# Padding three SBUF pools of a two-layer encoder so that matmul operands begin at multiples of 512 bytes

## The chip, the cores and the metric

The kernel runs on one core of one Trainium2 chip. The metric is the device time of one execution in microseconds (us), here the median of three runs. [...]

## The reference

Two layers, each a half-step SwiGLU, a mixer, and another half-step SwiGLU, on 512 tokens of 1024 values in float32:

```python
for l in range(DEPTH):                                   # DEPTH = 2
    x = x + 0.5 * swiglu_ffn(rmsnorm(x, ffn1_norm[l]), ffn1_w_up[l], ffn1_w_down[l])
    x = x + mixer(rmsnorm(x, mix_norm[l]), w_in[l], ...)
    x = x + 0.5 * swiglu_ffn(rmsnorm(x, ffn2_norm[l]), ffn2_w_up[l], ffn2_w_down[l])
    x = rmsnorm(x, final_norm[l])

def swiglu_ffn(h, w_up, w_down):                         # 1024 -> 2 x 2816 -> 1024
    a, b = jnp.split(h @ w_up, 2, axis=-1)
    return (jax.nn.silu(a) * b) @ w_down
```

The mixer makes one projection of 8704 columns (q, k, v of three groups of eight heads, a gated input of a convolution, two branch gates), runs a banded attention in each group, a depthwise convolution over 31 tokens with LayerNorm, a projection of each branch, their gated sum and an output projection.

## The kernel before

The activations are kept transposed, 128 channels on the partitions and 512 tokens along the free dimension, in eight tiles `x0` to `x7`. A float32 product is made of three products of parts rounded to `float32r`: `mm3` (lines 165 to 168) multiplies upper by upper, upper by lower and lower by upper part, into one PSUM bank. `nc.tensor.matmul(ps, a, b)` loads `a` as the stationary operand (the LDWEIGHTS rows on PEld) and streams `b` past it (the MATMUL rows on PE).

The weights come through `stage` (lines 152 to 163): a DMA on the SP queue into `raw`, a rounded copy `hi` on ScalarE (line 161), and `lo` = raw - hi on VectorE (line 162). They are tiles of 128 x 1024 of the pool `wp`, sliced in steps of 128 or 256 columns, that is of 512 or 1024 bytes. The streamed operands of 512 columns are whole tiles:

- `xgh`, `xgl` (the normalized input of an FFN or a mixer) and `zh`, `zl` in the pool `xp`. They are streamed in the up-projections (`ps_a`, `ps_b`), the gated input (`ps_ga`, `ps_gg`), the gates (`ps_gc`, `ps_gA`) and the convolution's projection (`ps_cp`);
- `sh`, `sl` in the pool of the FFN, or of the mixer, streamed in the down-projections (`ps_d`) and the attention's projection (`ps_ap`);
- `sgc` (upper) and `ml` (lower part of the merged branches) in the mixer's pool, streamed in the output projection (`ps_o`).

For q, k and v (`tokens_chunk`, lines 320 to 337) it is the other way round: slices of 128 columns of `xgh`, `xgl` are stationary, and 256 columns of `hi` or `lo` are streamed into `ps_n`, 24 matmuls and one of the bias (line 336) for every 128 tokens. The attention transposes tiles by matmuls with the identity `ident` as the streamed operand (lines 396 and 479).

Pools take SBUF in the order in which they are opened, each behind the last, and a pool's tiles stand one behind the other in the order in which their tags first come: `const` (identity, ones, small parameters, masks, `sel`), `xp`, `wp`, `rp` (small rows and columns, `R`), and then one at a time the pool `x0` of the start, the pool of each FFN and the pool `mp` of each mixer. The tiles `tmp`, `rt3`, `big` and `gqk` stand at the start of `mp`; behind `trash` come `tab`, `bias`, `qk`, `sgc`, `V`, `ot` and `sp`. All of these but `trash` are whole multiples of 512 bytes.

The order of the instructions on each engine is fixed when the program is built, by priorities and a simulated timeline; `stage` runs ahead of its use. On TensorE the work of the attention, the gates and the projections is mixed in that order.

Of the kernel before, what the change touches and what calls it, by code (L numbers as in the profile page):

```python
# [11 lines left out]
F32 = mybir.dt.float32  # L12
# [4 lines left out]
PSUM = bass.MemoryType.PSUM  # L17
DRAM = bass.MemoryType.DRAM

P = 128  # L20
# [5 lines left out]
HD = 64  # L26
# [5 lines left out]
CW = 31  # L32
CH = 256            # columns of q, k or v at a time: four heads
UH = CH // HD
FF = 2816
# [9 lines left out]
def trunk(ctx: ExitStack, tc: tile.TileContext, A: dict, out: bass.AP):  # L45
    nc = tc.nc
    const = ctx.enter_context(tc.tile_pool(name="const", bufs=1))
    xp = ctx.enter_context(tc.tile_pool(name="xp", bufs=1))
    wp = ctx.enter_context(tc.tile_pool(name="wp", bufs=4))
    rp = ctx.enter_context(tc.tile_pool(name="rp", bufs=2))  # L50
# [11 lines left out]

# [1 line left out]
    ident = const.tile([P, P], F32, name="ident")  # L64
# [7 lines left out]

    # input, natural layout
    x0s = ExitStack()
# [35 lines left out]
    nc.gpsimd.dma_start(sel32, A["sel"])  # L110
    sel = const.tile([96, 4, P], F32R, name="sel")
    nc.vector.tensor_copy(sel, sel32)
    # the biases of q, k, v as rows of three parts, in DRAM
    NB3 = DEPTH * 3 * AW // CH
# [29 lines left out]

# [1 line left out]
    cnt = [0]  # L146

    def uniq(s):
        cnt[0] += 1
        return f"{s}_{cnt[0]}"  # L150

    def stage(src):
        """Weights [128, a, n] into their upper and lower 12 bits."""
        a, n = src.shape[1], src.shape[2]
        raw = wp.tile([P, 1024], F32, tag="raw", name=uniq("raw"), bufs=2)
        hi = wp.tile([P, 1024], F32R, tag="hi", name=uniq("hi"))
        lo = wp.tile([P, 1024], F32R, tag="lo", name=uniq("lo"))
        m = a * n
        with tc.high_priority(offset=150):
            nc.sync.dma_start(raw[:, :m].rearrange("p (a n) -> p a n", a=a), src)  # L160
            nc.scalar.activation(hi[:, :m], raw[:, :m], AF.Copy)  # L161
            nc.vector.tensor_sub(lo[:, :m], raw[:, :m], hi[:, :m].bitcast(F32))  # L162
        return (hi[:, :m].rearrange("p (a n) -> p a n", a=a), lo[:, :m].rearrange("p (a n) -> p a n", a=a))
# [6 lines left out]
    def split(pool, src, tag, bufs):  # L170
        """A tile's upper and lower 12 bits."""
        return split_to(pool.tile([P, S], F32R, tag=tag, name=uniq("sh"), bufs=bufs), pool.tile([P, S], F32R, tag=tag, name=uniq("sl"), bufs=bufs), src)
# [39 lines left out]
    def broadcast_psum(rc, pool):  # L212
        """[128 tokens, 4] columns as a row over all partitions."""
        dg = pool.tile([P, S], F32, tag="tmp", name=uniq("dg"), bufs=7)
        for tt in range(TT):
            nc.vector.tensor_scalar_mul(dg[:, tt * P:(tt + 1) * P], ident, rc[:, tt:tt + 1])
        ps = ps_st(uniq("ps_bc"))
        nc.tensor.matmul(ps, ones, dg, start=True, stop=True)
        return ps
# [7 lines left out]
    def proj_cols(src, c0, rhs, nk, ps):  # L227
        """ps[j] = src[:, c0 + 128 j ..].T @ rhs, one or two tiles of columns."""
        nj = len(ps)
        step = 8 // nj  # L230
        for kk in range(0, nk, step):
            n_ = min(step, nk - kk)
            wh, wl = stage(src[:, kk:kk + n_, c0:c0 + nj * P])
            for j in range(nj):
                for k in range(n_):
                    kg = kk + k
                    mm3(ps[j], wh[:, k, j * P:(j + 1) * P], wl[:, k, j * P:(j + 1) * P], *rhs[kg], kg == 0, kg == nk - 1)

# [1 line left out]
    def ffn(l, w_up, w_down, xg, R, after, deferred=None):  # L240
# [30 lines left out]

# [1 line left out]
    def mixer(l, xg, R, rc, after):  # L273
# [5 lines left out]
        with ExitStack() as mx:  # L279
            mp = mx.enter_context(tc.tile_pool(name=uniq("mix"), bufs=2))  # L280
# [3 lines left out]

            # 1 / r as a row of three parts, and eps / r^2
            rr, rt = rc
            e4 = rp.tile([P, TT], F32, tag="e4", name=uniq("e4"))
            nc.vector.scalar_tensor_tensor(e4, rt, EPS, rt, op0=ALU.mult, op1=ALU.mult)
            ps = ps_st(uniq("ps_rt"))
# [8 lines left out]

# [1 line left out]
            u = [None] * KD  # L300
# [15 lines left out]

# [1 line left out]
            # one set of tables for the logarithms and the exponentials that follow  # L318
            tc.keep_in_program_order(nc.scalar.preload_act_table_set("natural_log_exp_and_others"))
            def tokens_chunk(c0):  # L320
                """256 columns of z over r, tokens on partitions: two PSUM banks of two tiles of tokens."""
                ps = [ps_mm(uniq("ps_n")) for _ in range(2)]
                w = [stage(win[:, kk:kk + 4, c0:c0 + CH]) for kk in (0, 4)]
                b3 = mp.tile([3, CH], F32R, tag="bias", name=uniq("bias"), bufs=2)
                nc.gpsimd.dma_start(b3, bd[(l * 3 * AW + c0) // CH])
                for tt in range(TT):
                    ts = slice(tt * P, (tt + 1) * P)
                    o = ps[tt // 2][:, (tt % 2) * CH:(tt % 2 + 1) * CH]
                    for k in range(KD):
                        wh, wl = w[k // 4][0][:, k % 4], w[k // 4][1][:, k % 4]  # L330
                        xh, xl = xg[k]
                        nc.tensor.matmul(o, xh[:, ts], wh, start=k == 0, stop=False)  # L332
                        nc.tensor.matmul(o, xh[:, ts], wl, start=False, stop=False)  # L333
                        nc.tensor.matmul(o, xl[:, ts], wh, start=False, stop=False)  # L334
                    # the bias, over the scale that the rows still lack
                    nc.tensor.matmul(o, rt3[:, ts], b3, start=False, stop=True)  # L336
                return ps

            # q carries the scores' factor, k its sign: the scores come out negated
            gqk = mp.tile([P, 2, NG, HD], F32, tag="gqk", name=uniq("gqk"), bufs=1)  # L340
            for i, (nm, f) in enumerate((("q_norm", SCALE), ("k_norm", -1.0))):
# [3 lines left out]
                nc.vector.tensor_scalar_mul(gqk[:, i], gqk[:, i], f)  # L345
            trash = mp.tile([P, HD], F32, tag="trash", name=uniq("trash"), bufs=1)

# [8 lines left out]
            def qk_chunk(g, hh, qk, tab):  # L356
                """Norm, rotation and transpose of four heads of q (0) or k (1): [2 x 64, pair of heads, positions]."""
                dil = DILS[g]
# [19 lines left out]
                for i in range(2):  # L378
                    nc.vector.tensor_mul(four(p2[i])[:, :, :, :32], four(zt[i])[:, :, :, 32:], tab[:, 1, tts[i], None, :32].to_broadcast([P, 2, UH, 32]))
                    nc.vector.tensor_mul(four(p2[i])[:, :, :, 32:], four(zt[i])[:, :, :, :32], tab[:, 1, tts[i], None, 32:].to_broadcast([P, 2, UH, 32]))  # L380
                    nc.vector.tensor_mul(four(p1[i]), four(zt[i]), tab[:, 0, tts[i], None, :].to_broadcast([P, 2, UH, HD]))
                # 1 / sqrt(v), polished by a Newton step
                nc.vector.scalar_tensor_tensor(v, v, 1.0 / HD, e4[:, :, None].to_broadcast([P, TT, UH]), op0=ALU.mult, op1=ALU.add)
# [20 lines left out]
            def v_chunk(g, hh):  # L404
                """v by way of DRAM: shifted by 64 tokens, or in the order of a group's positions."""
                ps = tokens_chunk(2 * AW + g * AOW + hh * CH)
# [24 lines left out]

            # by group and pair of heads, in the order of tokens: the outputs, and the negated maxima and denominators
            od = drp.tile([NG, 4, P, S], F32, tag="od", name=uniq("od"), bufs=1)
            sd = drp.tile([S, NG, 2, 2 * UH], F32, tag="sd", name=uniq("sd"), bufs=1)

            def attend(g, hh, qT, kT, V):
# [6 lines left out]
                for b2 in range(0, 4, 2):  # L443
                    po = ps_at(uniq("ps_pv"))
                    pv = po.rearrange("p (i b q) -> p i b q", i=2, b=2)
                    for bs in ([[b2], [b2 + 1]] if g == 0 else [[b2, b2 + 1]]):
                        lo, hi = 0, n
                        if g == 0:
                            lo, hi = (64 if bs[0] == 0 else 0), (192 if bs[0] == 3 else 256)
                        # a bank for the even and one for the odd heads: their row tiles run side by side  # L450
                        pS = [ps_at(uniq("ps_S")) for _ in range(2)]
# [7 lines left out]
                        for e in range(2):  # L459
# [4 lines left out]
                            if hi < n:  # L464
                                nc.vector.memset(sv[:, :, hi:], 0.0)
                            # the scores are negated, and so is the maximum
                            for w, (b, i) in enumerate(work):
# [46 lines left out]

# [1 line left out]
            sgc = []  # L516
# [21 lines left out]

# [1 line left out]
            cv = []  # L540
# [29 lines left out]

# [1 line left out]
            sa = slot("tmp", 7, name="sa")[:, :TT * NG * 4 * UH].rearrange("p (t g h s) -> p t g h s", t=TT, g=NG, h=2)  # L572
# [66 lines left out]

# [1 line left out]
    # the input, transposed  # L641
    ps = ps_st(uniq("ps_g"))
# [98 lines left out]

# [1 line left out]
def constants():  # L743
# [8 lines left out]
    m2 = np.where(i[:, None] // 32 == i[None, :] // 32, 0.0, POS)  # L752
    # rows 32 g + h: the partitions of head h among those of its pair
    sel = np.zeros((96, 4, P))
# [31 lines left out]
```

## Time and profile before

| | |
|---|---|
| three runs | 2724.01, 2725.06, 2725.06 us; median 2725.06 |
| span of the profiled execution, first to last instruction | 2723.4 us |
| granted TensorE clock over the span | 0.998 |
| PE busy | 2704.4 us (99% of the span), 14013 matmuls |
| PEld busy | 2242.8 us (82%) |
| VectorE (DVE) busy | 1536.0 us (56%) |
| ScalarE (ACT) busy | 1148.1 us (42%) |

A matmul's record in the profile runs from its start to a modelled end and overlaps the next one; how fast matmuls follow each other is read from the distance between two starts, which is called the pitch below. The profile gives no time of the profiled execution other than its span; the median of the runs is 1.7 us above it.

### The profile page before, as it was taken

The page shows a single profiled execution, that of the slowest core. Times are in us where ns is not written, and L with a number is a line of the kernel's source. Part 1 is how long each engine was busy: PE and PEld are TensorE (multiplying, and loading weights), DVE is VectorE, ACT ScalarE, POOL GpSimd, SP SyncE. Part 2 cuts the span into 40 slices and gives each one's busy share as a digit, 9 for nine tenths or more (in the row PEclk, how much of TensorE's full clock was granted, in tenths as well). Part 3 has the DMA queues.
Part 4 walks back from the last instruction along what each step waited for, and adds up shares of the span by engine and source line. Part 5 has one row for each costly group of instructions (what it writes and reads, how often), then busy time and mean ns, then how long its engine had stood idle before and what let it go on. Part 6 is the DMA issues. An engine that isn't in the chain of part 4 may idle for free.

```text
span 2723.4 us, 35608 instructions
## 1 busy us (share of the span) xinstructions
PE 2704.4 (99%) x14013; PEld 2242.8 (82%) x14013; DVE 1536.0 (56%) x2543; ACT 1148.1 (42%) x2457; POOL 149.6 (5%) x275
## 2 busy tenths in 40 slices
PE   8999999999999999999999999999999999999998
PEld 6888888988887788888888888889888877888887
DVE  4443344888888754443454434458888876434432
ACT  5232232656677343232333222335567773322322
POOL 2000000111120000000000000001111200000000
PEclk9999999999999999999999999999999999999999
DMA  4232233223233323322333333322322333333322
GB/s 157 93 101 91 93 98 94 88 87 98 86 101 104 123 89 98 100 93 93 93 94 100 94 95 94 99 91 87 96 86 87 106 107 116 93 101 93 101 89 74
DMA packets 260455, 264.50 MB, mean 97 GB/s; under 512 B 12542, under 2 KB 251742, under 8 KB 260288
## 3 DMA queue, kind: packets, MB, share of 16 engines
q1 hardware_dynamic: 247488, 234.91, 27.9%
q0 software_dynamic: 12784, 27.32, 3.3%
q8 instruction: 110, 1.80, 0.3%
q14 instruction: 57, 0.47, 0.1%
q10 hardware_dynamic: 16, 0.00, 0.0%
HBM read 247.18 MB, written 14.99 MB: 96 GB/s over the span
## 4 chain that ended last, share of the span: by engine, by line
PE 97%; ACT 1%; DVE 1%; DMA 0%; issue 0%; SPq 0%; ACTq 0%
PE ps_n L332 6%; PE ps_d L167 6%; PE ps_d L166 6%; PE ps_d L168 6%; PE ps_a L167 6%; PE ps_b L166 6%; PE ps_a L168 6%; PE ps_b L168 6%; PE ps_b L167 6%; PE ps_a L166 6%; PE ps_n L333 5%; PE ps_n L334 5%; PE ps_n L336 2%; PE ps_pv L487 2%; PE ps_S L457 1%; PE ps_T L479 1%
## 5 line engine op out<-in xcount | busy, mean ns | idle before, releaser
L162 DVE TENSOR_TENSOR lo<-raw,hi 128x1024 fp32r<-128x1024 f32 (+1 forms) x448 | 539.4, 1204 | 797.1 <-ACT hi L161 795.6
L161 ACT ACTIVATE hi<-raw 128x1024 fp32r<-128x1024 f32 (+1 forms) x448 | 467.7, 1044 | 970.6 <-issue 353.8
L332 PE MATMUL ps_n<-hi,xgh 128*128 128x256 f32 x1152 | 343.5, 298 | 0.0
L549 DVE SCALAR_TENSOR_TENSOR cv<-u,cwc,cv 128x497 f32<-128x497 f32 (+14 forms) x480 | 335.7, 736 | 0.1
L333 PE MATMUL ps_n<-lo,xgh 128*128 128x256 f32 x1152 | 330.1, 287 | 0.0
L334 PE MATMUL ps_n<-hi,xgl 128*128 128x256 f32 x1152 | 328.6, 285 | 0.0
L168 PE MATMUL ps_d<-sh,lo 128*128 128x512 f32 x704 | 277.4, 394 | 0.0
L166 PE MATMUL ps_d<-sh,hi 128*128 128x512 f32 x704 | 277.4, 394 | 0.0
L167 PE MATMUL ps_d<-sl,hi 128*128 128x512 f32 x704 | 277.4, 394 | 0.0
L167 PE MATMUL ps_b<-xgl,hi 128*128 128x512 f32 x704 | 275.5, 391 | 0.0
L167 PE MATMUL ps_a<-xgl,hi 128*128 128x512 f32 x704 | 274.1, 389 | 0.1
L168 PE MATMUL ps_a<-xgh,lo 128*128 128x512 f32 x704 | 274.1, 389 | 0.0
L166 PE MATMUL ps_b<-xgh,hi 128*128 128x512 f32 x704 | 273.9, 389 | 0.0
L168 PE MATMUL ps_b<-xgh,lo 128*128 128x512 f32 x704 | 273.9, 389 | 0.0
L166 PE MATMUL ps_a<-xgh,hi 128*128 128x512 f32 x704 | 273.3, 389 | 0.3 <-ACT xgh L183 0.3
L332 PEld LDWEIGHTS ps_n<-hi,xgh 128*128 128x128 f32 x1152 | 219.4, 190 | 21.4 <-issue 2.8
L333 PEld LDWEIGHTS ps_n<-lo,xgh 128*128 128x128 f32 x1152 | 220.0, 191 | 3.9 <-issue 3.6
L334 PEld LDWEIGHTS ps_n<-hi,xgl 128*128 128x128 f32 x1152 | 219.9, 191 | 2.4 <-issue 2.1
L166 PEld LDWEIGHTS ps_d<-sh,hi 128*128 128x128 f32 x704 | 131.7, 187 | 32.6
L168 PEld LDWEIGHTS ps_d<-sh,lo 128*128 128x128 f32 x704 | 131.6, 187 | 32.6
L167 PEld LDWEIGHTS ps_d<-sl,hi 128*128 128x128 f32 x704 | 131.7, 187 | 32.6
L168 PEld LDWEIGHTS ps_b<-xgh,lo 128*128 128x128 f32 x704 | 132.2, 188 | 28.3 <-issue 1.0
(247 smaller groups left out, 4276.5 us busy)
## 6 DMA issues: line engine op xcount, KB each, us to landing
raw<-in_ffn_w_up_dram SPq DMA_DIRECT2D x176, 512.0 KB, 3.5
raw<-in_w_in_dram SPq DMA_DIRECT2D x136, 512.0 KB, 3.6
raw<-in_ffn_w_down_dram SPq DMA_DIRECT2D x76, 512.0 KB, 3.4
raw<-in_w_conv_proj_dram SPq DMA_DIRECT2D x16, 512.0 KB, 3.4
raw<-in_w_out_dram SPq DMA_DIRECT2D x16, 512.0 KB, 3.5
vd<-tmp POOLq DMA_DIRECT2D x24, 256.0 KB, 2.7
od<-ot POOLq DMA_DIRECT2D x24, 256.0 KB, 3.0
oin<-od POOLq DMA_DIRECT2D x24, 256.0 KB, 3.0
```

Source lines behind the costliest of these rows:

```text
L161: nc.scalar.activation(hi[:, :m], raw[:, :m], AF.Copy)
L162: nc.vector.tensor_sub(lo[:, :m], raw[:, :m], hi[:, :m].bitcast(F32))
L166: nc.tensor.matmul(ps, ah, bh, start=first, stop=False)
L167: nc.tensor.matmul(ps, ah, bl, start=False, stop=False)
L168: nc.tensor.matmul(ps, al, bh, start=False, stop=last)
L332: nc.tensor.matmul(o, xh[:, ts], wh, start=k == 0, stop=False)
L333: nc.tensor.matmul(o, xh[:, ts], wl, start=False, stop=False)
L334: nc.tensor.matmul(o, xl[:, ts], wh, start=False, stop=False)
L336: nc.tensor.matmul(o, rt3[:, ts], b3, start=False, stop=True)
L457: nc.tensor.matmul(pS[e][:, w * n + lo:w * n + hi], qT[hp, i, b * P:(b + 1) * P], kT[hp, i, k0 + lo:k0 + hi], start=True, stop=True)
L487: nc.tensor.matmul(pv[e * 64:(e + 1) * 64, i, b - b2, :], V[b + j][:, h * HD:(h + 1) * HD], PT[e][:, (nj * w + j) * P:(nj * w + j + 1) * P ...
L549: nc.vector.scalar_tensor_tensor(a[:, t0:t1], u[k][:, t0 + d:t1 + d], cw(l, j, k), a[:, t0:t1], op0=ALU.mult, op1=ALU.add)
```

## The change

Three pools get bytes that nothing reads or writes: 40 floats (160 bytes) at the end of `const`, 80 floats (320 bytes) in `rp`, and `trash` in `mp` becomes 128 floats wide instead of 64, of which the first 64 are used as before (256 bytes more). Every tile behind a pad moves by it. The diff also takes out comments and docstrings, which are left out here.

```diff
@@ -109,8 +109,10 @@
     sel = const.tile([96, 4, P], F32R, name="sel")
+    const.tile([P, 40], F32, name="pad1")
+    rp.tile([P, 80], F32, tag="pad", name="pad2", bufs=1)
     nc.vector.tensor_copy(sel, sel32)
@@ -332,18 +334,18 @@
-            trash = mp.tile([P, HD], F32, tag="trash", name=uniq("trash"), bufs=1)
+            trash = mp.tile([P, 2 * HD], F32, tag="trash", name=uniq("trash"), bufs=1)[:, :HD]
```

## Rows read from the trace of the kernel before

**Rows 1.** The page: busy time, the granted clock, the chain that ended last.
```profile
PE 2704.4 (99%) x14013; PEld 2242.8 (82%) x14013; DVE 1536.0 (56%) x2543; ACT 1148.1 (42%) x2457; POOL 149.6 (5%) x275
...
PEclk9999999999999999999999999999999999999999
...
PE 97%; ACT 1%; DVE 1%; DMA 0%; issue 0%; SPq 0%; ACTq 0%
```

**Rows 2.** Waits of PE, longest first: total us, times, longest us.
```profile
PE ps_x L649 <- DMA xnat<-in_x_dram: 6.3, 1, 6.3
...
PE ps_cp L166 <- DVE sga L535: 0.8, 2, 0.4
```

**Rows 3.** Groups of PE by form: count, busy us, mean ns, idle before.
```profile
L332 PE MATMUL ps_n<-hi,xgh 128*128 128x256 f32 x1152 | 343.5, 298 | 0.0
...
L168 PE MATMUL ps_d<-sh,lo 128*128 128x512 f32 x704 | 277.4, 394 | 0.0
...
L168 PE MATMUL ps_cp<-zh,lo 128*128 128x512 f32 x128 | 49.6, 390 | 0.0
...
L166 PE MATMUL ps_ap<-sh,hi 128*128 128x512 f32 x64 | 25.2, 394 | 0.0
```

**Rows 4.** Timeline of PE, up-projection: start us, us; first and last of 30.
```profile
149.80 0.39 PE L166 MATMUL ps_a<-xgh,hi 128*128 128x512 f32 x1
...
156.37 0.39 PE L168 MATMUL ps_a<-xgh,lo 128*128 128x512 f32 x1
```

**Rows 5.** Timeline of PE, down-projection, first and last of 30.
```profile
299.69 0.39 PE L168 MATMUL ps_d<-sh,lo 128*128 128x512 f32 x1
...
306.45 0.39 PE L167 MATMUL ps_d<-sl,hi 128*128 128x512 f32 x1
```

**Rows 6.** Timeline of PE, tokens_chunk, first and last of 20.
```profile
471.62 0.28 PE L333 MATMUL ps_n<-lo,xgh 128*128 128x256 f32 x1
...
473.90 0.28 PE L334 MATMUL ps_n<-hi,xgl 128*128 128x256 f32 x1
```

**Rows 7.** Timeline of PE: transposes at either clock level, and one-column sums.
```profile
10.40 4.05 PE L649 MATMUL ps_x<-ident,xnat 128*128 128x128 f32 x18
...
22.07 1.03 PE L649 MATMUL ps_x<-ident,xnat 128*128 128x128 f32 x8
...
1005.99 0.95 PE L202 MATMUL ps_ss<-ones,sq 128*128 128x1 f32 x8
```

**Rows 8.** Durations of these two, by tile: ns min/median/max.
```profile
L649 PE MATMUL ps_x<-ident,xnat x32: 270/421/473, 9.9 to 24.1; 128*128 128x128 f32 x32
...
L202 PE MATMUL ps_ss<-ones,sq x72: 165/250/271, 389.5 to 2713.7; 128*128 128x1 f32 x72
```

**Rows 9.** Timeline of all engines, down-projection: a matmul and the next weight load.
```profile
300.39 0.39 PE L168 MATMUL ps_d<-sh,lo 128*128 128x512 f32 x1
300.39 0.19 PEld L166 LDWEIGHTS ps_d<-sh,hi 128*128 128x128 f32 x1
```

**Rows 10.** Timeline of PE around a broadcast between up-projection matmuls.
```profile
1012.55 0.40 PE L166 MATMUL ps_b<-xgh,hi 128*128 128x512 f32 x1
1012.78 1.02 PE L218 MATMUL ps_bc<-dg,ones 128*128 128x512 f32 x2
...
1013.88 0.40 PE L168 MATMUL ps_b<-xgh,lo 128*128 128x512 f32 x1
...
1014.35 0.39 PE L167 MATMUL ps_b<-xgl,hi 128*128 128x512 f32 x1
```

**Rows 11.** Stretches, first mixer: length, then busy us (count) of PE, PEld, DVE, ACT, POOL.
```profile
471.00:772.00 301.00, 301.00 (x2314) 268.04 (x2312) 254.25 (x556) 191.54 (x706) 41.78 (x73) 1.00 0.29 88
772.00:830.00 58.00, 58.00 (x328) 45.65 (x328) 54.59 (x118) 42.87 (x91) 12.92 (x25) 1.00 0.35 105
```

**Rows 12.** Groups and DMA issues of the weight staging, from the page.
```profile
L162 DVE TENSOR_TENSOR lo<-raw,hi 128x1024 fp32r<-128x1024 f32 (+1 forms) x448 | 539.4, 1204 | 797.1 <-ACT hi L161 795.6
...
raw<-in_ffn_w_up_dram SPq DMA_DIRECT2D x176, 512.0 KB, 3.5
```

## The prediction

> **What bounds the kernel now.** The page comes first: PE is busy 99% of the span, it had the upper clock level (2.4 GHz) but for the very start, and the chain that ended last is PE to 97% [rows 1]. The waits of PE say the same from the other side: 6.3 us at the start for the input, and later waits of about a microsecond at most, as before `ps_cp` [rows 2]. So the time is the sum of the pitches of the matmuls, and a change that adds no instruction can only act by these, or by making something else late.
>
> The groups of PE by form show that matmuls of one shape, 128x512, come in two kinds [rows 3]: `ps_cp` shows 390 ns, `ps_ap` and `ps_d` 394. In the whole list those that stream `xgh`, `xgl`, `zh`, `zl` from the pool `xp` are of the first kind, those that stream `sh`, `sl`, `sgc`, `ml` of the second. `ps_cp` and `ps_ap` come from the same function with the same shapes and weights and differ only in the streamed tile's pool. The timeline gives the pitch. Up-projection: 29 steps in 156.37 - 149.80 = 6.57 us, 226.6 ns [rows 4]. Down-projection: 6.76 us, 233.1 ns [rows 5]. With 256 columns: 19 steps in 2.28 us, 120.0 ns [rows 6].
>
> From the first and last of these: 106.6 ns for 256 columns more, 0.4164 ns a column, one column per cycle of 2.4 GHz. 512 columns then take 213.2 ns, and what is left is a part that doesn't depend on the columns: **13.4 ns** (32 cycles) in the up-projection and for 256 columns, **19.9 ns** (48 cycles) in the down-projection.
>
> **Where the operands begin.** The pads give it away. If 160 bytes behind `const` bring what follows to a multiple of 512, then `xp`, `wp` and `rp` now begin at 512 - 160 = 352 past one; with 320 more in `rp`, the FFN's and the mixer's pools begin at 512 - 480 = 32; behind `trash` it is 32 + 256 = 288. So the weights `hi`, `lo` and the streamed `xgh`, `xgl`, `zh`, `zl` begin at 352, that is 96 past a multiple of 128; `sh`, `sl` at 32 and `sgc`, `ml` at 288, both 32 past one. The short pitch goes with 96, the long one with 32, whether at 32 or at 288. Where an operand begins, in itself or against the weights loaded beside it, has a price. No row shows a `float32r` operand at a multiple of 128, so what remains of the 13.4 and 19.9 ns there must be bounded.
>
> **The change part by part.** It removes no instruction, adds none and moves none in time: the pads have no reader or writer, and `trash` keeps its 64 columns. The cost of the 736 bytes is nothing. What it moves are addresses:
>
> Three sets of matmuls get new ones. A: 352 to 0, 512 columns: `ps_a` and `ps_b` 6 x 704, and `ps_ga`, `ps_gg`, `ps_gc`, `ps_gA`, `ps_cp` 15 x 128, together 6144. B: 32 or 288 to 0: `ps_d` 3 x 704, `ps_o` 3 x 128, `ps_ap` 3 x 64, together 2688. C: 256 columns, `ps_n` 3 x 1152; of each 24 the first and last stand beside the bias, so 22 of 24 count, 3168.
>
> Bounds of the fixed part at 0. Above: it stays (13.4 ns; for B 19.9). Below: it goes, 0. The nearest rows are the transposes, whose streamed `ident` stands ahead of the pads; counted back from the end of `const` it begins 128 past a multiple of 512. At the low clock level 18 of them take (4.05 - 0.42)/17 = 213.5 ns each [rows 7, 8], half of which is 106.8; at the upper level 8 of them take (1.03 - 0.27)/7 = 108.6. Fixed part: 1.8 ns, at plain float32. I take that value. A 512-column matmul then has 213.2 + 1.8 = 215.0 ns.
>
> - A: 6144 x (226.6 - 215.0 = 11.6) = 71.3 us; bounds 0 and 6144 x 13.4 = 82.3.
> - B: 2688 x (233.1 - 215.0 = 18.1) = 48.7 us; bounds 0 and 53.5.
> - C: here the weight load comes close. One-column sums, where PE does little else than load 128x128 weights, follow each other in (0.95 - 0.165)/7 = 0.112 us [rows 7, 8]. So from 120.0 to 112: 3168 x 8.0 = 25.3 us; bounds 0 and 13.4 x 3168 = 42.5.
>
> Sum 145.3 us. **What gives some of it back:** VectorE. In the first mixer it is busy 254.25 of 301 us and then 54.59 of 58 us [rows 11]. C saves 12.7 us of the first stretch and the 192 gate matmuls 2.2 us of the second; DVE's share becomes 88% and 98%. Between no loss (PE waits for DVE 0.8 us in all now [rows 2]) and the loss of all 14.9 us per layer I stay near the row: 4 us per layer, 8 in all. The staging stays hidden: 24 matmuls per pair of weights give it 24 x 215 = 5.2 us, of which DVE needs 1.2; the landing takes 3.5 with two `raw` buffers [rows 12]. What becomes of DVE, ACT or DMA times at the new addresses no row shows; a few per cent of them hide behind PE in the FFNs, and in the 58 us stretch a 3% slower DVE would cost some 2 us per layer.
>
> So 145.3 - 8 = 137 off the span of 2723.4: 2586, and with the 1.7 us by which the median lies above it, **2588 us**.
>
> **The rivals.**
>
> 1. Part of the fixed cost goes. 48 and 32 cycles stand 16 apart; the next value would be 16 (6.7 ns). A 41.2, B 13.2 x 2688 = 35.5, C 21.2, less 3 for DVE: 95 us, 2630 us. For: the step of the two kinds is just that, and the 1.8 ns come from float32, which streams a column in two cycles where `float32r` takes one.
>
> 2. Only the two kinds become equal. If what counts is where the streamed tile stands against the weights (A: both at 352; B: 32 against 352), then after the change all are like A: 6.5 x 2688 = 17.5 us, 2707 us. For: a weight load begins within 0.01 us of a matmul and runs beside it [rows 9]; and a matmul of A beside which `ones` (also 128 past a multiple of 512) is loaded has the longer record, 0.40 against 0.39 us [rows 10]. Against: that load is plain float32.
>
> 3. The change doesn't do what it says: 2725 us. Every tile already begins at a multiple of 32 bytes (352, 32, 288), and if nothing coarser counts, the new addresses are as good as the old ones and the 6.5 ns between the two kinds have another cause. Against: `ps_cp` and `ps_ap` share all but the streamed tile's pool [rows 3]. [...]
>
> 4. Slower. Weight load and stream, both now starting at a multiple of 512 in the same instant [rows 9], meet at the same place all the way. That the two can get in each other's way shows where their rhythm is broken: behind a broadcast two steps take 0.47 us, where two of the steady stream take 0.45 [rows 4, 10]. If all go to the 19.9 ns of B: 6.5 x (6144 + 3168) = 60.5 us, 2785 us. It decides from a fixed part of 14.9 ns on, the mean of today's over the 12,000 matmuls. [...]
>
> **How the numbers follow.** The forecast (the fixed part nearly gone, 2547 to 2610): 0.42. Rival 1 (2610 to 2690): 0.17. Rival 2: 0.17. Rival 3: 0.07. Rival 4: 0.17. A difference under 0.2% (5.5 us) can't be told from none here. Faster: 0.42 + 0.17 + 0.17 = 0.76; same 0.07; slower 0.17. The lower end is the bound at which everything goes: 82.3 + 53.5 + 42.5 = 178.3, 2547 us, which DVE makes unlikely; I put it at 2552. The upper end takes in rival 2 and, to leave out no more than 2 in 10, rival 3: 2726. The forecast's own range is 2552 to 2610.
>
> **What the changed profile would show.** The same count of instructions. The distance of starts in `ps_a`, `ps_d` and `ps_n`: 215, 215 and 112 ns by the forecast; 220, 220, 113 by rival 1; 227, 227, 120 by rival 2; unchanged by rival 3; 233, 233 and 127 by rival 4. All say that the two kinds become one but rival 3: if `ps_d` and `ps_a` still differ, where a tile begins was not the cause. DVE near 98% behind 765 us in the first mixer, with PE waits of some us for `sgc` or `hi`, would show the loss that I priced at 8 us; waits of PE for `raw` or `lo` in an FFN would prove the staging wrong. The prediction fails outright if the fixed part belongs to `float32r` and its weight load rather than to the place.

## The result and the profile after

The changed kernel takes 2705.77 us (median of 4 runs, 2705.64 to 2705.88) against 2724.97 us (the kernel before, with a fourth run), a ratio of 0.993 with a 95% interval of 0.9916 to 0.9944. It is 0.7% faster, not 5%.

The page of the changed kernel, busy time and chain, answers to [rows 1]:

```profile
span 2703.9 us, 35608 instructions
...
PE 2684.4 (99%) x14013; PEld 2244.4 (83%) x14013; DVE 1535.6 (57%) x2543; ACT 1148.2 (42%) x2457; POOL 149.6 (6%) x275
...
PE 98%; ACT 1%; DVE 0%; DMA 0%; issue 0%; SPq 0%; ACTq 0%
```

The instructions are as many as before, and TensorE (PE) sets the end as before; 20.0 us of its busy time are gone. The groups of PE by form (count, busy us, mean ns, idle before) say where, against [rows 3]:

```profile
L334 PE MATMUL ps_n<-hi,xgh 128*128 128x256 f32 x1152 | 343.6, 298 | 0.0
...
L170 PE MATMUL ps_d<-sh,lo 128*128 128x512 f32 x704 | 274.0, 389 | 0.0
...
L170 PE MATMUL ps_cp<-zh,lo 128*128 128x512 f32 x128 | 49.6, 390 | 0.0
...
L168 PE MATMUL ps_ap<-sh,hi 128*128 128x512 f32 x64 | 24.9, 389 | 0.0
```

The two kinds have become one: `ps_d` and `ps_ap` fell from 394 to 389 ns, `ps_cp` and `ps_n` stayed. The timeline of PE, first and last of 30, then of 30, then of 21 matmuls, and a matmul beside which another tile is loaded, answers to [rows 4, 5, 6, 10]:

```profile
148.77 0.39 PE L169 MATMUL ps_a<-xgl,hi 128*128 128x512 f32 x1
...
155.34 0.39 PE L168 MATMUL ps_a<-xgh,hi 128*128 128x512 f32 x1
...
298.82 0.39 PE L168 MATMUL ps_d<-sh,hi 128*128 128x512 f32 x1
...
305.40 0.39 PE L170 MATMUL ps_d<-sh,lo 128*128 128x512 f32 x1
...
467.45 0.28 PE L334 MATMUL ps_n<-hi,xgh 128*128 128x256 f32 x1
...
469.85 0.28 PE L336 MATMUL ps_n<-hi,xgl 128*128 128x256 f32 x1
...
1006.08 0.40 PE L168 MATMUL ps_b<-xgh,hi 128*128 128x512 f32 x1
1006.31 1.02 PE L220 MATMUL ps_bc<-dg,ones 128*128 128x512 f32 x2
```

The pitch in `ps_a` is 6.57 us / 29 = 226.6 ns, exactly that of before; in `ps_d` 6.58 / 29 = 226.9, where it was 233.1; in `ps_n` 2.40 / 20 = 120.0, as before. So the part that doesn't depend on the columns is 13.4 to 13.7 ns in all of them, with every operand at a multiple of 512. A cycle is here the time of one column, 0.4164 ns as worked out from [rows 4, 6]; its inverse is the prediction's 2.4 GHz, an estimate that takes a column for a cycle, since the profile lists the clock as a share alone (a mean of 0.998 before and 1.000 after). The last two rows show what was already seen before: beside the load of `ones`, which stands 128 past a multiple of 512, a matmul whose streamed tile stands at 0 has the longer record, 0.40 us against 0.39. That matmul's own weights stand at 0 as well; only the tile loaded beside it doesn't. This hints that the load beside the stream counts and not the weights in use, but it is one kind of row: in e2 below, with the streamed tile at 32, the same record is 0.39 us. In every steady stream of the runs both stand at the same distance, so they don't part the two.

Of the span's 19.5 us, set B gives 2688 x 6.66 ns = 17.9 (an estimate: 560 and 544 cycles of 0.4164 ns are 233.2 and 226.5 ns, and the pitches of all these rows, 226.6 to 226.9 and 233.1, lie within 0.4 ns of them). The wait for the input at the start gives 0.6 more (5.7 us, where [rows 2] has 6.3). The last 1.0 us is in `ps_n`. PE's busy time for that tile alone, in a window that holds all its matmuls, in the kernel before and after (length, busy, count, granted clock, DMA share, GB/s):

```profile
460.00:2150.00 1690.00, 514.79 (x3600) 1.00 0.31 95
...
460.00:2150.00 1690.00, 513.84 (x3600) 1.00 0.31 96
```

By their records, half of this is in the bias matmuls (55.0 to 54.5 us); the cause stays open.

### The profile page after: what moved, and what is told of

Its sections match the earlier page's. It is cut to its first block, busy times and chain, and to the rows that moved or that the text cites. A ratio compares the mean times of both kernels' runs of the same rounds, so it can differ in the third digit from the quotient of the medians.

```text
span 2703.9 us, 35608 instructions
## 1 busy us (share of the span) xinstructions
PE 2684.4 (99%) x14013; PEld 2244.4 (83%) x14013; DVE 1535.6 (57%) x2543; ACT 1148.2 (42%) x2457; POOL 149.6 (6%) x275
## 4 chain that ended last, share of the span: by engine, by line
PE 98%; ACT 1%; DVE 0%; DMA 0%; issue 0%; SPq 0%; ACTq 0%
PE ps_n L334 6%; PE ps_a L168 6%; PE ps_b L168 6%; PE ps_a L170 6%; PE ps_d L170 6%; PE ps_a L169 6%; PE ps_b L170 6%; PE ps_d L168 6%; PE ps_b L169 6%; PE ps_d L169 6%; PE ps_n L335 5%; PE ps_n L336 5%; PE ps_n L338 2%; PE ps_pv L489 2%; PE ps_S L459 1%; PE ps_T L481 1%
## 5 line engine op out<-in xcount | busy, mean ns | idle before, releaser
L169 PEld LDWEIGHTS ps_b<-xgl,hi 128*128 128x128 f32 x704 | 132.2, 188 | 28.1 <-issue 1.0
L168 PEld LDWEIGHTS ps_a<-xgh,hi 128*128 128x128 f32 x704 | 132.3, 188 | 27.8 <-ACT xgh L185 0.7
L169 PEld LDWEIGHTS ps_a<-xgl,hi 128*128 128x128 f32 x704 | 132.3, 188 | 27.6 <-DVE xgl L186 0.3
```

The source lines that it names most:

```text
L168: nc.tensor.matmul(ps, ah, bh, start=first, stop=False)
L169: nc.tensor.matmul(ps, ah, bl, start=False, stop=False)
```

## The experiments

Two theories stood at the start. **Place**: what counts is where the streamed tile begins by itself; 0 and 96 past a multiple of 128 are good, 32 is bad. **Distance**: what counts is where it stands against the weights that are loaded beside it; a distance is the difference of the two places. Both fit the change. All edits below are on the changed kernel.

**e1_equal_352**, all operands at 352:

```diff
-    const.tile([P, 40], F32, name="pad1")
```

> The pad behind const is left out, the other two stay: streamed tiles and weights all begin at 352 past a multiple of 512. Distance theory (only where the streamed tile stands against the weights loaded beside it counts): pitch 226.6 ns in ps_a and ps_d, and the time of the change, 2706 us. Place theory (the streamed tile's own place counts; 0 and 96 past a multiple of 128 cost 13.4 ns, 32 past costs 19.9): the same, 2706 us. If the multiple of 512 itself mattered: slower than 2706 us.

Measured: 2706.16 us, ratio 0.9931 (0.9914 to 0.9948). Timeline of PE, down-projection, first and last of 30:

```profile
298.70 0.39 PE L168 MATMUL ps_d<-sl,hi 128*128 128x512 f32 x1
...
305.27 0.39 PE L167 MATMUL ps_d<-sh,hi 128*128 128x512 f32 x1
```

226.6 ns. The multiple of 512 is not needed, and of the three pads the one behind `const` does nothing here. It doesn't part the two theories.

**e2_equal_32**, all operands at 32:

```diff
-    const.tile([P, 40], F32, name="pad1")
+    const.tile([P, 48], F32, name="pad1")
```

> The pad behind const grows by 32 bytes: streamed tiles and weights all begin at 32 past a multiple of 512. Distance theory: pitch 226.6 ns everywhere, 2706 us. Place theory: every streamed tile stands where the slow ones of before stood, pitch 233.1 ns everywhere and about 127 ns for 256 columns, about 2780 us.

Measured: 2705.8 us, 0.9929 (0.9915 to 0.9944). Timeline of PE, down-projection, first and last of 30:

```profile
298.84 0.39 PE L170 MATMUL ps_d<-sh,lo 128*128 128x512 f32 x1
...
305.41 0.39 PE L169 MATMUL ps_d<-sl,hi 128*128 128x512 f32 x1
```

226.6 ns, at the place at which `ps_d` had 233.1 before the change. The place theory is out: it wanted about 2780 us.

**e3_pad1_only**, the pad behind `const` alone, which brings `xp` and `wp` to 0 and the FFN's and the mixer's pools 64 past a multiple of 128:

```diff
-    rp.tile([P, 80], F32, tag="pad", name="pad2", bufs=1)
-            trash = mp.tile([P, 2 * HD], ...)[:, :HD]
+            trash = mp.tile([P, HD], ...)
```

> Only the pad behind const: weights and the tiles of xp at 0, the FFN's and the mixer's streamed tiles at 192 and 448, that is 64 past a multiple of 128. Distance theory: ps_a 226.6 ns; ps_d, ps_o and ps_ap stand 64 from the weights modulo 128 as before the change, 233 ns, about 2724 us. Place theory: no row has a tile at 64; between the neighbours 32 (19.9 ns) and 96 (13.4), so 226.6 to 233.1 ns, 2706 to 2724 us.

Measured: 2725.4 us, ratio 1.0002 (0.9993 to 1.0011): the whole gain is gone. Timeline, first and last of 30:

```profile
298.77 0.39 PE L167 MATMUL ps_d<-sh,hi 128*128 128x512 f32 x1
...
305.53 0.39 PE L169 MATMUL ps_d<-sh,lo 128*128 128x512 f32 x1
```

6.76 / 29 = 233.1 ns, as the distance theory says; the place theory allowed it too.

**e4_sweep**, pairs of `xp` 32 bytes further each:

```diff
         src = xs[k] if src is None else src
+        if k and k not in shifted:
+            shifted.add(k)
+            xp.tile([P, 8], F32, tag=f"shift{k}", name=f"shift{k}")
         hi = xp.tile([P, S], F32R, tag=f"xgh{k}", name=uniq("xgh"))
```

> Each pair xgh, xgl of xp begins 32 bytes further past a multiple of 512 than the one ahead: 0, 32, ... 224; weights and all other streamed tiles at 224. Distance theory: in ps_a the pitch is 226.6 ns for the pairs 3 and 7 (0 or 128 from the weights), 233 ns for 1 and 5 (64 away), in between or unlike for 0, 2, 4 and 6. Place theory: 226.6 ns for pairs 0, 3, 4, 7, 233 ns for 1 and 5. ps_d 226.6 ns by both.

Measured: 2737.39 us, ratio 1.0045 (1.0029 to 1.0061). Groups of PE by form:

```profile
L171 PE MATMUL ps_a<-xgh,lo 128*128 128x512 f32 x704 | 278.2, 395 | 0.0
...
L170 PE MATMUL ps_d<-sl,hi 128*128 128x512 f32 x704 | 273.9, 389 | 0.0
```

`ps_d`, all at 224 like the weights, keeps 389. `ps_a` goes to 395 as a whole, near the long kind, though only two of its eight pairs stand 64 away. Neither theory's pattern came out. The steps within a pair scatter from 225 to 238 ns, so a reading by pair would settle nothing. If every distance but 0 costs 6.66 ns, seven of eight pairs lose 5376 x 6.66 = 36 us. By PE's busy time, tile by tile, the matmuls that stream from `xp` are 32.9 us busier than in the changed kernel and `ps_n` 1.3 us less (512.54 us); the sum is the 31.6 us measured. So on average a distance other than 0 costs nearly the full 6.66 ns. That made **equality** the next theory.

**e5_distances**, steady streams at three other distances:

```diff
-    rp.tile([P, 80], F32, tag="pad", name="pad2", bufs=1)
+    rp.tile([P, 88], F32, tag="pad", name="pad2", bufs=1)
-            rt3 = slot("rt3", 1, F32R)[:3, :]
+            rt3 = mp.tile([P, S + 24], F32R, tag="rt3", ...)[:3, :S]
-            trash = mp.tile([P, 2 * HD], ...)[:, :HD]
+            trash = mp.tile([P, 2 * HD + 24], ...)[:, :HD]
```

> From the changed kernel on, the pads in rp, rt3 and trash grow: weights and the tiles of xp stay at 0, the streamed tiles of the down-projection go to 32, those of the attention's projection to 128, those of the output projection to 224 (96 past a multiple of 128). Distance theory with a period of 128 bytes: ps_ap 226.7 ns as at distance 0; ps_d and ps_o something between 226.7 and 233.3, equal to each other if the cost is even in the distance, 2706 to 2724 us. A ramp (48 cycles at 64, 32 at 0, 40 between) gives 230 ns and 2714 us. If equality is the whole rule and any other distance costs the same: 233.3 in ps_d and ps_o, ps_ap too if the period is longer, 2724 us.

Measured: 2724.13 us, ratio 0.9997 (0.9988 to 1.0007). Timeline, first and last of 30 at distance 32, then of 24 at 128:

```profile
298.73 0.40 PE L168 MATMUL ps_d<-sh,hi 128*128 128x512 f32 x1
...
305.50 0.39 PE L170 MATMUL ps_d<-sh,lo 128*128 128x512 f32 x1
...
930.01 0.40 PE L168 MATMUL ps_ap<-sh,hi 128*128 128x512 f32 x1
...
935.37 0.39 PE L170 MATMUL ps_ap<-sh,lo 128*128 128x512 f32 x1
```

233.4 and 233.0 ns. At 224 the output projection has the long records too (group by form):

```profile
L170 PE MATMUL ps_o<-sgc,lo 128*128 128x512 f32 x128 | 50.6, 395 | 0.0
```

There is no ramp, and 128 is as bad as 32: on the average of a steady stream, places are either equal or not.

**e7_distance_256** asks for the period:

```diff
-    rp.tile([P, 80], F32, tag="pad", name="pad2", bufs=1)
+    rp.tile([P, 144], F32, tag="pad", name="pad2", bufs=1)
```

> From the changed kernel on, the pad in rp grows by 256 bytes: weights and the tiles of xp at 0, all streamed tiles of the FFN's and the mixer's pool at 256. If streamed tile and weights have to be equal modulo 256: 226.7 ns in ps_d, ps_o and ps_ap, 2706 us. If equal modulo 512 (no less): 233.3 ns, 2688 x 6.6 ns = 18 us more, 2724 us.

Measured: 2705.91 us, ratio 0.9931 (0.9911 to 0.9951); first and last of 30:

```profile
298.70 0.39 PE L170 MATMUL ps_d<-sh,lo 128*128 128x512 f32 x1
...
305.27 0.39 PE L169 MATMUL ps_d<-sl,hi 128*128 128x512 f32 x1
```

226.6 ns. Equal modulo 256 bytes is enough.

**e8_weights_off** turns the change's own words against it: every streamed tile stays at a multiple of 512.

```diff
+    wp.tile([P, 8], F32, tag="shift", name="shift", bufs=1)
-    rp.tile([P, 80], F32, tag="pad", name="pad2", bufs=1)
+    rp.tile([P, 72], F32, tag="pad", name="pad2", bufs=1)
```

> From the changed kernel on, the weights' pool wp is moved by 32 bytes and the pad in rp cut by 32: every streamed tile stays at 0, only the weights stand at 32. Equality theory: 233.3 ns in all 8832 matmuls of 512 columns, 59 us more than the change, 2764 us. Place theory (streamed operands at multiples of 512 are what counts): 2706 us, no difference.

Measured: 2753.46 us, ratio 1.0105 (1.0088 to 1.0122). Timeline, first and last of 30 in an up-projection, then of 22 in `tokens_chunk`:

```profile
149.71 0.40 PE L170 MATMUL ps_b<-xgl,hi 128*128 128x512 f32 x1
...
156.48 0.39 PE L169 MATMUL ps_a<-xgh,hi 128*128 128x512 f32 x1
...
480.20 0.28 PE L337 MATMUL ps_n<-hi,xgl 128*128 128x256 f32 x1
...
482.66 0.28 PE L337 MATMUL ps_n<-hi,xgl 128*128 128x256 f32 x1
```

With the same streamed places all 512-column matmuls are at 233.4 ns. The time is 11 us under what was expected, and the lower rows show why: with 256 columns, unequal places are *faster*, 2.46 / 21 = 117.1 ns instead of 120.0. PE's busy time for `ps_n` shows what that is worth over the whole run:

```profile
460.00:2150.00 1690.00, 506.73 (x3600) 1.00 0.30 95
```

Against the 513.84 us of the changed kernel that is 7.1 of the 11 us. The 512-column matmuls are 55.7 us busier where 59 were expected; the gates `ps_gc` and `ps_gA`, between which other work is mixed, fall short the most.

**e9_short_streams** and **e10_unequal** ask how the price goes with the columns, **e6_short_loads** how it goes with the loaded weights. In each, `proj_cols` shortens the matmuls of two projections, all but those of the first and last channel tile (the tiles of 128 input channels that a product is summed over); e10 also takes the three pads out. The edit, shortened here (e6 has `cols` alone):

```diff
-def proj_cols(src, c0, rhs, nk, ps):
+def proj_cols(src, c0, rhs, nk, ps, cols=P, toks=S):
...
+                    w, n = (P, S) if kg in (0, nk - 1) else (cols, toks)
-                    mm3(ps[j], wh[:, k, j * P:(j + 1) * P], wl[...], *rhs[kg], ...)
+                    mm3(ps[j][:w, :n], wh[:, k, j * P:j * P + w], wl[...], *[t[:, :n] for t in rhs[kg]], ...)
```

> From the changed kernel on (all equal), the down-projection's matmuls but those of the first and last channel tile stream 384 tokens instead of 512, the output projection's 320; the other tokens' products are left out. Fixed part (32 cycles a matmul, whatever the columns): 160.0 + 13.3 = 173.3 ns and 133.3 + 13.3 = 146.7 ns. A rate (one cycle lost in 16 columns): 170.0 and 141.7 ns.

> The kernel before with its places (streamed 32 or 288, weights 352). Down-projection: 384 tokens streamed but in the first and last channel tile; output projection: 64 columns of weights loaded but there; the rest of these products is left out. Fixed part of 48 cycles: 180.0 ns in ps_d; a rate of 48 in 512: 175.0 ns. If a short load costs more only because it gives back less at equal places (48 cycles less one for 8 loaded columns): 233.3 ns in ps_o, as with 128 columns loaded; if the load takes time from the stream in any place: under 233.3.

> From the changed kernel on, in the down-projection all matmuls but the first and last channel tile load 64 columns of weights instead of 128, in the output projection 32: the products of the other columns are left out. All stream 512 columns as before. If the 13.4 ns left over are what the load of the next weights takes from the stream: they shrink with the loaded columns, ps_d to 220 ns and ps_o to 217 ns. If they are a price of each matmul (a hand-over or a start): 226.7 ns in both.

Their times (2582.14, 2610.92 and 2714.46 us for e9, e10 and e6) are those of less work and don't compare; only the steps do. Timeline of e9 (equal places), first and last of 20 with 384 columns and of 14 with 320:

```profile
290.84 0.33 PE L169 MATMUL ps_d<-sl,hi 128*128 128x384 f32 x1
...
294.13 0.33 PE L170 MATMUL ps_d<-sh,lo 128*128 128x384 f32 x1
...
925.47 0.31 PE L168 MATMUL ps_o<-sgc,hi 128*128 128x320 f32 x1
...
927.37 0.31 PE L169 MATMUL ps_o<-ml,hi 128*128 128x320 f32 x1
```

173.2 and 146.2 ns: at equal places a fixed 13 ns. Timeline of e10 (unequal), first and last of 20 with 384 columns, then of 15 with 512 columns and 64 columns of weights loaded:

```profile
290.80 0.34 PE L166 MATMUL ps_d<-sh,hi 128*128 128x384 f32 x1
...
294.11 0.34 PE L167 MATMUL ps_d<-sl,hi 128*128 128x384 f32 x1
...
928.27 0.39 PE L166 MATMUL ps_o<-sgc,hi 128*64 128x512 f32 x1
...
931.53 0.40 PE L168 MATMUL ps_o<-sgc,lo 128*64 128x512 f32 x1
```

174.2 ns for 384 columns, near the rate's 175.0 and far from the 180.0 of a fixed part; 232.9 with short loads, near the 233.1 of long ones. Timeline of e6 (equal), first and last of 30 with 64 loaded columns, then of 9 with 32:

```profile
293.16 0.39 PE L170 MATMUL ps_d<-sh,lo 128*64 128x512 f32 x1
...
299.83 0.39 PE L169 MATMUL ps_d<-sl,hi 128*64 128x512 f32 x1
...
961.69 0.39 PE L168 MATMUL ps_o<-sgc,hi 128*32 128x512 f32 x1
...
963.55 0.40 PE L170 MATMUL ps_o<-sgc,lo 128*32 128x512 f32 x1
```

6.67 / 29 = 230.0 and 1.86 / 8 = 232.5 ns, against 226.7 with 128. The second is over eight steps alone and good to about 1 ns. Neither expectation held: a shorter load makes the stream slower, not faster, and drives it towards the value of unequal places. What is left at equal places is no toll that grows with the load. Nor do the loads' own records (PEld, by form; 188 ns with 128 columns) show another kind of load:

```profile
L168 PEld LDWEIGHTS ps_d<-sh,hi 128*64 128x64 f32 x640 | 86.2, 135 | 58.1
...
L168 PEld LDWEIGHTS ps_o<-sgc,hi 128*32 128x32 f32 x96 | 10.4, 109 | 10.0
```

From 188 to 135 to 109 ns is 0.8 ns a column in both steps.

**e11_qkv_off** and **e12_qkv_at_0** put what was learned to use: the 256-column matmuls unequal, the 512-column ones equal. Both have the longer weight tiles and two buffers of `V` less; they differ in `8` against `0`.

```diff
-    def stage(src):
+    def stage(src, c=0):
-        hi = wp.tile([P, 1024], F32R, tag="hi", name=uniq("hi"))
-        lo = wp.tile([P, 1024], F32R, tag="lo", name=uniq("lo"))
+        hi = wp.tile([P, 1024 + 64], F32R, tag="hi", name=uniq("hi"))[:, c:c + 1024]
+        lo = wp.tile([P, 1024 + 64], F32R, tag="lo", name=uniq("lo"))[:, c:c + 1024]
-                w = [stage(win[:, kk:kk + 4, c0:c0 + CH]) for kk in (0, 4)]
+                w = [stage(win[:, kk:kk + 4, c0:c0 + CH], 8) for kk in (0, 4)]
-                    v = mp.tile([P, CH], F32, tag="V", name=uniq("V"), bufs=10)
+                    v = mp.tile([P, CH], F32, tag="V", name=uniq("V"), bufs=8)
```

> From the changed kernel on, the tiles hi and lo get 64 more columns (256 bytes, so they still begin at 0 modulo 256), V two buffers fewer (8) for the room, and the weights of q, k and v are put 32 bytes into their tiles: the 256-column matmuls have streamed and loaded operand unequal, all 512-column ones equal. If unequal places cost a share of the columns (the 116.9 ns for 256 columns seen with the weights moved) and equal ones a fixed 13.3 ns: 116.9 in ps_n, 226.7 in the others, about 11 us under the change, 2695 us. If ps_n was faster there for another reason: 119.6 ns, 2706 us.

> The same sizes and buffers, but the weights of q, k and v at the start of their tiles: all equal. 119.6 ns in ps_n, 2706 us by both theories, if the two buffers of V cost nothing.

Measured: e12 2705.86 us, ratio to before 0.9931 (0.9918 to 0.9944), no different from the change; e11 **2698.66 us**, 0.9904 (0.989 to 0.9918), 7.2 us under e12 and the fastest kernel here that does all the work. Timeline of e11, `tokens_chunk`, first and last of 22:

```profile
467.43 0.28 PE L336 MATMUL ps_n<-hi,xgl 128*128 128x256 f32 x1
...
469.88 0.28 PE L336 MATMUL ps_n<-hi,xgl 128*128 128x256 f32 x1
```

2.45 / 21 = 116.7 ns. The expected 11 us were taken from the whole surplus in e8, of which `ps_n` had 7.1. Here its busy time is that of e8, against 513.82 us in e12:

```profile
460.00:2150.00 1690.00, 506.69 (x3600) 1.00 0.31 97
```

That is 7.1 us again, and all of the gain. The streamed place 32 by itself doesn't do it: in e2, where both operands stand at 32, `ps_n` is 513.69 us busy, as in the changed kernel.

## Why the prediction was wrong

**What bounds the kernel, and the two kinds:** right. The time is the sum of the pitches, the pads cost nothing, and the streamed tile's pool told the kinds apart. It is the pitch that tells them, though, and not, as the prediction has it, the mean record in the whole list: the gates stream from `xp` and have mean records of up to 404 ns, longer than the second kind's 394, before and after the change alike. From the kernel before:

```profile
L166 PE MATMUL ps_gc<-xgh,hi 128*128 128x512 f32 x128 | 51.7, 404 | 0.0
```

**The step that failed** is the one that put the fixed part at 1.8 ns ("The nearest rows are the transposes [...] I take that value"). For this value it looked at the place of the streamed operand alone, and it took a plain float32 transpose, which took 0.85 ns a column (108.6 ns for 128) where `float32r` took 0.4164, for a sample of `float32r` at a good place. The 106.8 ns it took off, half of the slow transposes' 213.5, was an estimate too: the profile of the kernel before lists a granted clock of 1.00 for their stretch (10.4 to 14.4 us) as for that of the fast ones (22.0 to 23.1 us), so no row shows that they ran at half the clock. The fixed part at a multiple of 512 is 13.4 to 13.7 ns, and 13.4 at 352 and at 32 too, wherever both operands stand alike (e1, e2). So A gave 0 of its 71.3 us and C 1.0 at most of its 25.3. B gave 17.9 of 48.7, the 6.5 ns between the kinds that were in the rows. The prediction's last sentence had named this way to fail: the fixed part does not belong to the place. That it belongs to the weight load, as that sentence goes on, no run shows (e6).

The 19.9 ns "that doesn't depend on the columns" were wrong as well. They came from 512 columns alone; at unequal places the part over 0.4164 ns a column grows with the columns (174.2 ns for 384 in e10, where a fixed part gives 180.0). Rival 1's ladder of 48, 32 and 16 cycles rests on the same reading.

The measured time lies far outside the forecast's own range of 2552 to 2610; it is in the wide one, to 2726, because that took in rivals 2 and 3.

**Rival 2** named what happened and its size, 2707 us. For it stood the row beside `ones` [rows 10] and the load that runs beside each matmul [rows 9]. I held against it that the load of `ones` is plain float32; e8 shows the longer step (233.4 ns against 226.6) with `float32r` weights moved by 32 bytes. With the rows at hand it deserved more than its 0.17: it was the only case that explained all the pitches without a value that no row had.

**Rival 1** (a step of 16 cycles down) failed with the forecast. **Rival 3** is out by e3 against e7, which differ in places alone. **Rival 4**, equal places as the worst case, had the sign wrong for 512 columns (226.6 ns at equal places, 233.0 to 233.4 at unequal ones). For 256 columns equal places are the slower ones (120.0 against 116.7 ns, e11), but they were equal before the change too, so that nothing rose to its 127 ns. That the place of the loaded operand bears on the stream, e8 does show: there a 32-byte move of the loaded operand alone lengthens the steady 512-column steps by 6.8 ns (226.6 to 233.4). What is lost there, no run shows.

**VectorE**, and with it the 8 us given back, was not put to the test, since little of the time went. (In the kernel before, PE's waits for it were not 0.8 us in all: `ps_ss` waited another 0.9 for `sq`.) Its stretches of the first mixer, to be held against [rows 11], are about as busy as they were (the same columns):

```profile
471.00:772.00 301.00, 301.00 (x2304) 267.75 (x2304) 255.17 (x556) 191.43 (x708) 42.51 (x74) 1.00 0.29 89
772.00:830.00 58.00, 58.00 (x330) 45.73 (x329) 54.22 (x119) 45.53 (x94) 12.21 (x24) 1.00 0.36 109
```

What stays open is the mechanism: why equal places turn a share of the columns into a fixed part, and why a shorter load takes part of that back. The runs show the dependence, not its cause.

## What to carry to other kernels

When two groups of equal `float32r` matmuls have different pitches, look at both operands: hold the streamed tile's address against that of the weights loaded beside it, modulo 256 bytes, before aligning either to anything. For streams of 512 columns make them equal (226.6 against 233.4 ns a matmul here, the change and e8), for 256 try them unequal (116.7 against 120.0 ns, e11 and the change). And a price that no row shows should not be taken from the row with the nicest address, when a difference between two rows already gives a case that needs no new price.

## What the runs showed of the hardware

- `float32r`, 128 columns of weights loaded beside each matmul, mean granted clock 0.998 to 1.000: at places equal modulo 256 bytes a matmul of 256, 320, 384 or 512 columns takes 120.0 (the change), 146.2, 173.2 (e9) and 226.6 ns (the change, e1, e2, e7), 0.4164 ns a column and some 13 ns. At unequal places 256, 384 and 512 take 116.7 and 117.1 (e11, e8), 174.2 (e10) and 233.0 to 233.4 ns (the kernel before, e3, e5, e8): about 9% over 0.4164 ns a column. Between 256 and 384 columns the two cross.
- At equal places a shorter load is dearer: 128, 64 and 32 loaded columns give 226.6 (the change), 230.0 and 232.5 ns (e6) for 512 streamed columns (the last over eight steps). At unequal places 128 and 64 give 233.1 (the kernel before) and 232.9 (e10).
- Streamed place less loaded place, modulo 256 bytes, was 32 and 128 (e5), 192 (the kernel before, e3), 224 (e5, e8) and 0 (the change, e1, e2, e7) in steady streams of 512 columns. Only 0 has the short step, 226.6 to 226.9 ns; the others have 233.0 to 233.4. 64, 96 and 160 occur in the mix of e4 alone.
